# Two-bank PSUM buffers already in the first mixer matmul, weight splits a tile earlier, sums at half pace, one conv-state load

## The chip, the cores and the metric

The kernel runs on one core of a Trainium2 chip. The metric is the device time of one execution in microseconds (us). Below, PE is TensorE (matmuls), DVE is VectorE, ACT is ScalarE, POOL is GpSimd and SP is the engine that issues most DMAs. A DMA can also be issued from the queue of ACT.

## The reference

One layer of a decoder is computed for 1024 prompt tokens and 8 x 4 sample tokens, with T = 1056 columns in all, 1024 features and 4096 hidden features:

```python
xn = rms_norm(x, norm1_g) * (1 + scale1) + shift1
h, b_gate, c_gate, q, k, v, g_conv, g_att = jnp.split(jnp.dot(xn, w_in), split_at, axis=-1)
u = c_gate * h                       # sample rows: the last two rows of state_conv stand ahead
y_conv = conv_w[0] * u_ext[:, 0:ns] + ...
conv_out = jnp.dot(b_gate * y_conv, w_conv_out)
...
attn_out = jnp.dot(o.reshape(nb, ns, D_ATT), w_attn_out)
mixed = jax.nn.sigmoid(g_conv) * conv_out + jax.nn.sigmoid(g_att) * attn_out
x = x + gate1 * jnp.dot(mixed, w_o)                      # output projection
xn2 = rms_norm(x, norm2_g) * (1 + scale2) + shift2
hid = jax.nn.relu(jnp.dot(xn2, w_mlp_in))                # first mixer matmul
x = x + gate2 * jnp.dot(hid * hid, w_mlp_out)            # second mixer matmul
```

## The kernel before

Everything is kept transposed: a tile has 128 features on the partitions and tokens along the row. To keep the precision of f32, each operand is split in a high and a low part, and each product is three matmuls: high by high, high by low and low by high. Raw weights come by DMA (`load_to`, issued on SP). `prep_to` makes the high part `whi` on ACT (L201) and the low part `wlo` on DVE (L208); with `lazy` the low part is put on a list of things due at the next `slot()`, the point after each tile at which pieces of background work are issued too.

The engines work at their own instruction streams, in the order in which the Python code emits them. The order of the work is thus that of the code, and a generator of background work (`bg`) gives up pieces with a cost each (`yield 300`), so many per slot as the `rate` allows.

The stages are, by time: the pair jobs of the conv and the gates (until about 500 us), attention (until 1200), the projections of conv and attention (until 1335), the output projection (`project`, 24 tiles of 24 matmuls with 352 columns, one of 8 feature blocks m by one of three column chunks ch), 12 plain tiles of the first mixer matmul (`plain_tiles`), 14 pair jobs of it, then the second mixer matmul.

A pair job (`pair_job`) computes two blocks of 128 output features by a seven-product scheme. Its seven passes n = 0 to 6 each multiply one combined weight `wprod` (split by ACT L166 and DVE L170, two passes ahead) with one quarter of the columns, in two halves p = 0 and 1 of 12 matmuls of 264 columns. Half 0 writes a PSUM tile `ps_g` (three buffers of one bank each), half 1 a tile `ps_s` (two buffers). After its 12 matmuls each half is read at once: by an ACT copy (L277 in pass 0, L282 in pass 2), by DVE into a sum (L284 in pass 3, L288 in pass 4) or by `fin`, which is a DVE sum (L1565), a relu and a square on ACT (L1566, L1567) in passes 1, 4, 5 and 6. In the code the readers of half 0 stand between the matmuls of half 0 and those of half 1.

After the last pair job `wide_banks` closes the pool of one-bank tiles and opens a pool of four tiles `ps_w` with two banks each; the second mixer matmul (L1738 to L1740) fills both halves of such a tile and then reads it once. That matmul's operands `hh` and `hl` (L1590, L1598) are prepared while the last pair job runs (`warm`).

For the first pair job in the mixer, sums and differences of the normalized input's quarters are formed by `sums`: DVE and POOL subtractions (L343, L344, L348, L350), and splits `th`, `tl` (L366). They run as background work while the plain tiles run.

The sample rows' conv state is loaded by eight small DMAs (L768), two for each of the first pair jobs' conv blocks, from the queue of SP.

Of the kernel before, what the change touches and what calls it, by code (L numbers as in the profile page):

```python
# [9 lines left out]
F32 = mybir.dt.float32  # L10
# [7 lines left out]
P = 128  # L18
T = 1056
NP = 1024  # L20
CH = 352
NCH = 3
KD = 8
NPC2 = NP - 2 * CH
H = 264
# [3 lines left out]
NB = 8  # L29
# [20 lines left out]
class Trunk:  # L50
    def __init__(self, ctx, tc, t):
        self.tc, self.nc, self.t = tc, tc.nc, t
        pool = lambda **kw: ctx.enter_context(tc.tile_pool(**kw))
        self.cp = pool(name="const", bufs=1)
        self.pg = pool(name="pages", bufs=NPG)
        self.ck = pool(name="chunks", bufs=8)
        self.wp = pool(name="weights", bufs=3)
        self.sm = pool(name="small", bufs=3)
        self.px = ExitStack()
        self.pp = self.px.enter_context(tc.tile_pool(name="psum", bufs=1, space=PSUM))  # L60
        self.dp = pool(name="scratch", bufs=1, space=DRAM)
        self.bg = deque()
        self.paced = [deque(), deque()]
        self.pause = [0, 0]
        self.credit = 0.0
        self.rate = 0.0
        self.items = deque()
        self.ready = set()
        self.bias = None
        self.done = False  # L70
        self.work = 0.0
        self.later = []
        self.act_load = 0.0
        self.dve_load = 0.0
# [15 lines left out]
    def wide_banks(self):  # L90
        self.px.close()
        self.pp = self.px.enter_context(self.tc.tile_pool(name="wide", bufs=1, space=PSUM))

    def wide(self):
        return self.pp.tile([P, 2, 512], F32, name="ps_w", tag="ps_w", bufs=4)
# [155 lines left out]
    def pair_job(self, i, fin, after=None):  # L251
        nc = self.nc
        n0 = 7 * self.npair
        self.npair += 1
        s, z = {}, {}
        for n in range(7):
            if n == 1 and i + 1 < len(self.srcs) and len(self.srcs[i + 1]) == 2:
                self.load_to(i + 1)
            if n == 5 and i + 1 < len(self.srcs) and len(self.srcs[i + 1]) == 1:
                self.load_to(i + 1)  # L260
            if n == 5:
                self.prep_to(i + 1)
            self.products_to(min(n0 + n + 3, self.last_prod))
            w = self.prods.popleft()
            if n == 2:
                self.need("T")
            for p in range(2):
                ps = self.bank("s" if p else "g")[:, :H]
                for k in range(4):
                    hi, lo = w[:, k * P:(k + 1) * P], w[:, 512 + k * P:512 + (k + 1) * P]  # L270
                    xh, xl = self.operand(n, k, p)
                    nc.tensor.matmul(ps, hi, xh, start=(k == 0), stop=False)  # L272
                    nc.tensor.matmul(ps, hi, xl, start=False, stop=False)  # L273
                    nc.tensor.matmul(ps, lo, xh, start=False, stop=(k == 3))  # L274
                if n == 0:
                    s[p] = self.chunk("ps_s")[:, :H]
                    nc.scalar.copy(s[p], ps)  # L277
                elif n == 1:
                    fin(0, 0, p, s[p], ps, ALU.add, False)
                elif n == 2:  # L280
                    z[p] = self.chunk("ps_z")[:, :H]
                    nc.scalar.copy(z[p], ps)  # L282
                elif n == 3:
                    nc.vector.tensor_tensor(out=s[p], in0=s[p], in1=ps, op=ALU.add)  # L284
                    nc.gpsimd.tensor_tensor(out=z[p], in0=z[p], in1=s[p], op=ALU.add)  # L285
                elif n == 4:
                    fin(1, 1, p, z[p], ps, ALU.add, False)
                    nc.vector.tensor_tensor(out=s[p], in0=s[p], in1=ps, op=ALU.add)  # L288
                elif n == 5:
                    fin(1, 0, p, s[p], ps, ALU.subtract, True)  # L290
                else:
                    fin(0, 1, p, z[p], ps, ALU.add, True)
                self.slot()
            del w
            if after is not None:
                after(n)

# [32 lines left out]
        k += 4 if n else 0  # L330
        return self.xh[k][:, c0:c0 + H], self.xl[k][:, c0:c0 + H]

    def sums(self):
        nc = self.nc
        self.tt = {}

        def quarters(k):
            return [v.rearrange("p (a t n) -> p a t n", a=2, t=2)[:, :, i] for v in (self.xp[k], self.xp[k + 4]) for i in range(2)]

        for step in range(6):  # L340
            if step < 4:
                b11, b12, b21, b22 = quarters(step)
                nc.vector.tensor_tensor(out=b11, in0=b12, in1=b11, op=ALU.subtract)  # L343
                nc.gpsimd.tensor_tensor(out=b12, in0=b22, in1=b12, op=ALU.subtract)  # L344
                yield 300
            if 1 <= step < 5:
                b11, b12, b21, b22 = quarters(step - 1)
                nc.vector.tensor_tensor(out=b22, in0=b22, in1=b11, op=ALU.subtract)  # L348
                yield 150
                nc.gpsimd.tensor_tensor(out=b21, in0=b22, in1=b21, op=ALU.subtract)  # L350
                yield 150
            k = step - 2
            if k < 0:
                continue
            x = self.xp[k], self.xp[k + 4]
            tt = []
            for i, v in enumerate(x):
                w = 2 * H if k == 3 and i == 0 else T
                h, l = [], []
                for c in range(0, T, w):  # L360
                    for d, n in ((h, "th"), (l, "tl")):
                        d.append(self.page(n, dt=F32R) if w == T else self.half(n, (P, w), F32R))
                    nc.scalar.copy(h[-1], v[:, c:c + w])
                yield 300
                for j, c in enumerate(range(0, T, w)):
                    nc.vector.tensor_tensor(out=l[j], in0=v[:, c:c + w], in1=h[j].bitcast(F32), op=ALU.subtract)  # L366
                tt.append((h, l))
                yield 300
            self.tt[k] = tt
            self.xp[k] = self.xp[k + 4] = None  # L370
        self.ready.add("T")
# [65 lines left out]
    def start(self):  # L437
        nc, t = self.nc, self.t
        c = self.cp
# [21 lines left out]
        self.load_to(0)  # L461
        load_x(2)
        self.load_to(1)
        self.b_ada, self.g1, self.g2 = vec[:, 0:48], vec[:, 48:56], vec[:, 56:64]
        self.cw = vec[:, 64:88].rearrange("p (a k) -> p a k", a=3)
        eps = c.tile([P, 2], F32, name="eps")
# [296 lines left out]
    def conv_h(self, m):  # L763
        u = self.u = [self.page("u", (P, NP + 2)) for _ in range(2)]
        us = self.us = [self.sm.tile([P, NB, 6], F32, name="us", tag="us", bufs=2) for _ in range(2)]
        for i in range(2):
            self.nc.vector.memset(u[i][:, 0:2], 0.0)
            self.nc.sync.dma_start(out=us[i][:, :, 0:2], in_=self.t["state_conv"][:, m + i])  # L768

        def fin(mi, t, p, a, ps, op, last):  # L770
            for dst, sl, four in self.parts(mi, t, p):
                x, y = a[:, sl], ps[:, sl]
                if four:
                    x, y = (v.rearrange("p (b t) -> p b t", t=NT) for v in (x, y))
                self.nc.vector.tensor_tensor(out=dst, in0=x, in1=y, op=op)
        return fin
# [518 lines left out]
    def run(self):  # L1295
        nc, t, c = self.nc, self.t, self.cp
# [51 lines left out]
        while len(jobs[ji]) == 2:  # L1348
            kd, m = jobs[ji]
# [25 lines left out]
        for ji in range(ji, nb):  # L1375
            kd, g, j = jobs[ji]
            for ch in range(NCH):
                s = slice(ch * CH, (ch + 1) * CH)
                ps = self.bank("g")
# [20 lines left out]
        base = nb  # L1400
# [15 lines left out]
        for n, (ch, m) in enumerate(seq):  # L1416
# [5 lines left out]
            ps = self.bank("g")  # L1422
# [15 lines left out]
        mixh, mixl = {}, {}  # L1438
# [3 lines left out]
        for n, (m, ch) in enumerate(seq):  # L1442
            s = slice(ch * CH, (ch + 1) * CH)
            i, x = divmod(m, 2)
# [15 lines left out]
            del ps, y  # L1460
            if x == 0 and ch == 0:
                self.prep_to(base + i + 1)
            if x == 1 and ch == 2:
                self.wt.pop(base + i)
            self.slot()
# [25 lines left out]
        def project(i, m, ch):  # L1491
            s = slice(ch * CH, (ch + 1) * CH)
            load_x1()
            self.prep_to(i + 1, True)
            ps = self.bank("g")
            self.gemm(ps[:, :CH], self.wt[i], range(KD), [(mixh[k, ch], mixl[k, ch]) for k in range(KD)])
            self.residual(x1[m], ps, gate1, m, ch)
            self.later.append((2, lambda: nc.sync.dma_start(out=self.x1_d[m][:, s], in_=x1[m][:, s])))

# [12 lines left out]
        for chs in ((0,), (1,), (2,)):  # L1512
# [6 lines left out]
            def tail(ch):  # L1519
# [12 lines left out]
                    yield 500  # L1532
                self.ready.add(("x2", ch))
                if ch == 2:
                    yield from self.sums()

            self.later.append((5, lambda chs=chs, tail=tail: self.bg.extend(tail(ch) for ch in chs)))
            for m in range(KD):
# [162 lines left out]
        self.rate = 1000.0  # L1701
        self.plain_tiles(base, "x2", hidden)
        self.last_prod = 7 * (self.npair + 2 * NBLK - NG // 2 + 2 * NSB)
        ji = base + NG
        for i in range(NG, 4 * NBLK, 2):
            if i + 6 < 4 * NBLK:
# [3 lines left out]
        for m in range(KD):  # L1710
            at(END - 11 + 2 * m, lambda m=m: load_y1(m))
            if m > 3:
                at(END + 13 + m, lambda m=m: store(m))
        self.wide_banks()
        g = 0
        for i in range(2 * NSB):
            b, x = divmod(i, 2)
# [266 lines left out]
```

## Time and profile before

| | |
|---|---|
| median of 3 runs | 2136.11 us (2134.2 to 2136.56) |
| the profiled execution | 2137.93 us, of which its span from first to last instruction 2136.1 us |
| busy: PE, DVE, ACT, POOL | 2022.3, 1412.4, 996.6, 780.6 us |
| TensorE clock granted, mean | 0.984 of full speed |
| output projection, 1335 to 1437 us | PE busy 95.7 of 102 us |
| plain tiles, 1437 to 1490 us | PE busy 49.2 of 53 us |
| mixer pair jobs, 1490 to 1776 us | PE busy 286 of 286 us |

The span is the time from the first to the last instruction of the execution; the rest of its time lies around it. A busy share is that of the time in which at least one instruction of the engine runs. Matmuls overlap each other, so the spacing of their starts says more than their length.

### The profile page before, as it was taken

To read this page: it belongs to the slowest core of one execution; us is meant where nothing else is said; L and a number is where in the kernel's file an instruction comes from. 1 tells how busy PE (TensorE), PEld (TensorE's weight loads), DVE (VectorE), ACT (ScalarE), POOL (GpSimd) and SP (SyncE) were. 2 spreads that over 40 slices of the span, in tenths; PEclk is the share of its full clock that TensorE was granted. 3 is DMA by queue.
4 is the path that set the end of the run, shared out by engine and by line. 5 is a ranking of instruction groups with operands and counts; after the bars stand their busy time and mean duration, and the time that the engine had idled before them with its cause. 6 is when DMAs were issued, how large, how long until landed. Compare 5 with 4: busy or idle time off the path is not lost. (4 is left out here: it accounts for less than half of the span.)

```text
span 2136.1 us, 38668 instructions
## 1 busy us (share of the span) xinstructions
PE 2022.3 (95%) x15092; PEld 1901.1 (89%) x15092; DVE 1412.4 (66%) x2776; ACT 996.6 (47%) x2165; POOL 780.6 (37%) x544
## 2 busy tenths in 40 slices
PE   5899999999999999999999989999999998999998
PEld 2799999889989888888888889989999998999998
DVE  4847766434667655566676677678444446999998
ACT  4623232434666655555555233455555556433332
POOL 3635655421111111100011114234333335888885
PEclk8899999999999999999999999999999999999999
DMA  7242312664122344333247985642356729555542
GB/s 288 64 144 83 101 51 91 220 233 160 47 65 61 119 130 132 122 126 123 88 141 233 284 261 181 202 158 86 135 192 246 258 102 356 180 202 207 209 149 115
DMA packets 143375, 338.68 MB, mean 159 GB/s; under 512 B 34392, under 2 KB 81112, under 8 KB 142168
## 3 DMA queue, kind: packets, MB, share of 16 engines
q1 hardware_dynamic: 142760, 336.01, 46.8%
q8 instruction: 118, 1.93, 0.4%
q14 instruction: 65, 0.53, 0.1%
q10 hardware_dynamic: 432, 0.20, 0.0%
HBM read 279.00 MB, written 116.39 MB: 185 GB/s over the span
## 5 line engine op out<-in xcount | busy, mean ns | idle before, releaser
L170 DVE TENSOR_TENSOR wprod<-wraw,wprod 128x512 fp32r<-128x512 f32 x276 | 276.0, 1000 | 179.8 <-ACT wprod L166 178.2
L385 PE MATMUL ps_g<-xh,whi 128*128 128x352 f32 x1056 | 357.0, 338 | 8.0 <-DVE graw L107 3.8
L385 PE MATMUL ps_g<-xh,wlo 128*128 128x352 f32 x1056 | 345.8, 328 | 7.2 <-DVE wlo L208 7.2
L385 PE MATMUL ps_g<-xl,whi 128*128 128x352 f32 x1056 | 345.8, 327 | 2.4 <-POOL xl L414 1.5
L1738 PE MATMUL ps_w<-hh,wprod 128*128 128x264 f32 x784 | 225.1, 287 | 13.7 <-DVE acc L1745 7.0
L385 PEld LDWEIGHTS ps_g<-xh,whi 128*128 128x128 f32 x1056 | 202.9, 192 | 32.9 <-issue 13.2
L1739 PE MATMUL ps_w<-hl,wprod 128*128 128x264 f32 x784 | 224.0, 286 | 0.0
L1740 PE MATMUL ps_w<-hh,wprod 128*128 128x264 f32 x784 | 223.9, 286 | 0.0
L166 ACT CAST wprod<-wraw 128x512 fp32r<-128x512 f32 x276 | 163.1, 617 | 123.6 <-DVE wprod L170 91.1
L385 PEld LDWEIGHTS ps_g<-xh,wlo 128*128 128x128 f32 x1056 | 202.4, 192 | 8.5 <-DVE wlo L208 8.5
L385 PEld LDWEIGHTS ps_g<-xl,whi 128*128 128x128 f32 x1056 | 203.4, 193 | 4.9 <-POOL xl L414 3.4
L208 DVE TENSOR_TENSOR wlo<-wraw,whi 128x512 fp32r<-128x512 f32 x200 | 151.7, 798 | 50.8 <-ACT whi L201 50.4
L170 POOL TENSOR_TENSOR lo<-qn,hi 128x1024 fp32r<-128x1024 f32 x12 | 32.9, 2738 | 360.6 <-ACT hi L166 325.0
L1738 PEld LDWEIGHTS ps_w<-hh,wprod 128*128 128x128 f32 x784 | 148.6, 190 | 15.4 <-issue 7.8
L285 POOL TENSOR_TENSOR ps_z<-ps_z,ps_s 128x264 f32<-128x264 f32 x64 | 63.9, 1000 | 255.4 <-DVE ps_s L284 255.3
L1740 PEld LDWEIGHTS ps_w<-hh,wprod 128*128 128x128 f32 x784 | 148.7, 190 | 0.0
L1739 PEld LDWEIGHTS ps_w<-hl,wprod 128*128 128x128 f32 x784 | 148.7, 190 | 0.0
L272 PE MATMUL ps_s<-th,wprod 128*128 128x264 f32 x512 | 146.3, 286 | 1.7 <-DVE ps_s L284 1.7
L272 PE MATMUL ps_g<-th,wprod 128*128 128x264 f32 x512 | 146.7, 287 | 0.0
L274 PE MATMUL ps_g<-th,wprod 128*128 128x264 f32 x512 | 145.9, 285 | 0.0
L273 PE MATMUL ps_s<-tl,wprod 128*128 128x264 f32 x512 | 145.7, 285 | 0.0
L273 PE MATMUL ps_g<-tl,wprod 128*128 128x264 f32 x512 | 145.7, 285 | 0.0
(351 smaller groups left out, 5936.9 us busy)
## 6 DMA issues: line engine op xcount, KB each, us to landing
wraw<-in_w_in SPq DMA_DIRECT2D x76, 512.0 KB, 4.3
wada<-in_w_ada SPq DMA_DIRECT2D x48, 512.0 KB, 5.4
hid_d<-hid SPq DMA_DIRECT2D x32, 528.0 KB, 3.4
wraw<-in_w_mlp_in SPq DMA_DIRECT2D x32, 512.0 KB, 5.8
wraw<-in_w_mlp_out SPq DMA_DIRECT2D x32, 512.0 KB, 3.8
hraw<-hid_d SPq DMA_DIRECT2D x56, 264.0 KB, 4.6
kv<-in_v SPq DMA_DIRECT2D x28, 512.0 KB, 6.1
wraw<-in_w_conv_out SPq DMA_DIRECT2D x24, 512.0 KB, 7.9
```

The source lines that it names most:

```text
L166: nc.scalar.copy(hi, src)
L170: eng.tensor_tensor(out=lo, in0=src, in1=hi.bitcast(F32), op=ALU.subtract)
L208: self.nc.vector.tensor_tensor(out=lo[:, s], in0=w[:, s], in1=hi[:, s].bitcast(F32), op=ALU.subtract)
L272: nc.tensor.matmul(ps, hi, xh, start=(k == 0), stop=False)
L273: nc.tensor.matmul(ps, hi, xl, start=False, stop=False)
L274: nc.tensor.matmul(ps, lo, xh, start=False, stop=(k == 3))
L285: nc.gpsimd.tensor_tensor(out=z[p], in0=z[p], in1=s[p], op=ALU.add)
L385: self.nc.tensor.matmul(ps, a, x, start=(i == 0), stop=(i == n - 1))
L1738: nc.tensor.matmul(ps[:, p], wh, xh, start=(k == 0), stop=False)
L1739: nc.tensor.matmul(ps[:, p], wh, xl, start=False, stop=False)
L1740: nc.tensor.matmul(ps[:, p], wl, xh, start=False, stop=(k == 1))
```

## The change

Five edits:

- In `pair_job` both halves of a pass write one two-bank tile `ps_w` if `self.joint` is set, which `wide_banks` now does. `wide_banks` is called ahead of the mixer's pair jobs, no longer behind them; the pair jobs of the conv stage run with `joint` unset.
- In `project` the weight of tile i + 2 is split in the middle of tile i (`gemm` calls `mid` after 12 of 24 matmuls); before, that of tile i + 1 was split ahead of tile i. One call in the stage before brings the first one.
- `sums` for the last chunk's tail charges its pieces twice the cost, so about half as many are emitted per slot.
- The conv state is loaded once, as `old`, by one DMA on the queue of ACT at the start; DVE copies take the place of the eight small loads.

```diff
     def wide_banks(self):
         self.px.close()
         self.pp = self.px.enter_context(self.tc.tile_pool(name="wide", bufs=1, space=PSUM))
+        self.joint = True
...
+            two = self.wide() if self.joint else None
             for p in range(2):
-                ps = self.bank("s" if p else "g")[:, :H]
+                ps = two[:, p, :H] if self.joint else self.bank("s" if p else "g")[:, :H]
                 for k in range(4):
...
-    def sums(self):
+    def sums(self, f=1):
...
-                yield 300
+                yield 300 * f
...
+        self.old = c.tile([P, KD, NB, 2], F32, name="old")
+        nc.scalar.dma_start(out=self.old, in_=t["state_conv"])
...
-            self.nc.sync.dma_start(out=us[i][:, :, 0:2], in_=self.t["state_conv"][:, m + i])
+            self.nc.vector.tensor_copy(us[i][:, :, 0:2], self.old[:, m + i])
...
+            if x == 1 and ch == 0 and i == 3:
+                self.prep_to(base + i + 2, True)
...
-            self.prep_to(i + 1, True)
             ps = self.bank("g")
-            self.gemm(ps[:, :CH], self.wt[i], range(KD), [(mixh[k, ch], mixl[k, ch]) for k in range(KD)])
+            self.gemm(ps[:, :CH], self.wt[i], range(KD), [(mixh[k, ch], mixl[k, ch]) for k in range(KD)],
+                      lambda: self.prep_to(i + 2, True))
...
-                    yield from self.sums()
+                    yield from self.sums(2)
...
         self.last_prod = 7 * (self.npair + 2 * NBLK - NG // 2 + 2 * NSB)
+        self.wide_banks()
...
-        self.wide_banks()
```

The first place that shows how instructions move is PE in pass n = 1 of a mixer pair job, where half 0 ends and half 1 begins. Names carry the number of their buffer; in brackets stands the engine whose semaphore the instruction waits on. Before:

```order
L272 MATMUL ps_g_17118<-xh_15185,wprod_17031 128x264
L273 MATMUL ps_g_17118<-xl_15193,wprod_17031 128x264
L274 MATMUL ps_g_17118<-xh_15185,wprod_17031 128x264
L272 MATMUL ps_s_17135<-xh_15182,wprod_17031 128x264 [waits DVE_49]
L273 MATMUL ps_s_17135<-xl_15190,wprod_17031 128x264
L274 MATMUL ps_s_17135<-xh_15182,wprod_17031 128x264
```

Half 1 opens another tile than half 0 filled; its wait is on the reader that emptied this buffer of `ps_s` two passes earlier. After:

```order
L275 MATMUL ps_w_17356<-xh_15187,wprod_17271 128x264
L276 MATMUL ps_w_17356<-xl_15195,wprod_17271 128x264
L277 MATMUL ps_w_17356<-xh_15187,wprod_17271 128x264
L275 MATMUL ps_w_17356<-xh_15184,wprod_17271 128x264 [waits DVE_49]
L276 MATMUL ps_w_17356<-xl_15192,wprod_17271 128x264
L277 MATMUL ps_w_17356<-xh_15184,wprod_17271 128x264
```

The same tile now stands on both sides. The wait's counter, followed through the built program, is that of the DVE instruction L1572 that reads half 0 of this same tile `ps_w_17356`, so half 1 begins after that read; in pass n = 0 and 2 the wait is on the ACT copy of half 0 in the same way.

The second place is DVE around that read. Before, in the order in which DVE runs them (the splits of the next products, then the two readers of this pass):

```order
L170 TENSOR_TENSOR wprod_17076<-ws1_17034,wprod_17076 128x512 [waits Activation_49]
L170 TENSOR_TENSOR wprod_17115<-wraw_16850,wprod_17115 128x512 [waits PE_49,Activation_49]
L1565 TENSOR_TENSOR ps_t_17131<-ps_s_17092,ps_g_17118 128x264 [waits PE_49]
L1565 TENSOR_TENSOR ps_t_17148<-ps_s_17108,ps_s_17135 128x264 [waits PE_49]
L170 TENSOR_TENSOR wprod_17152<-wraw_16852,wprod_17152 128x512 [waits DMAHW1_49,DVE_49,Activation_49]
```

After:

```order
L172 TENSOR_TENSOR wprod_17315<-ws1_17274,wprod_17315 128x512 [waits Activation_49]
L172 TENSOR_TENSOR wprod_17353<-wraw_17095,wprod_17353 128x512 [waits Activation_49]
L1572 TENSOR_TENSOR ps_t_17369<-ps_s_17331,ps_w_17356 128x264 [waits PE_49]
L1572 TENSOR_TENSOR ps_t_17385<-ps_s_17346,ps_w_17356 128x264 [waits PE_49]
L172 TENSOR_TENSOR wprod_17389<-wraw_17097,wprod_17389 128x512 [waits DMAHW1_49,DVE_49,Activation_49]
```

The order on DVE is the same; the two readers now read one tile, and the split of a later product still stands ahead of them.

The third place is DVE at the second-quarter sums and the first pair job (L343, L348 are the subtractions, L366 the `tl` splits, L208 the low parts of a plain tile's weight). Before:

```order
L366 TENSOR_TENSOR tl<-x_14843,th 128x1056
L343 TENSOR_TENSOR x_14803<-x_14803 128x2x264
L348 TENSOR_TENSOR x_14923<-x_14923,x_14765 128x2x264
L208 TENSOR_TENSOR wlo<-wraw,whi 128x512 x2
L366 TENSOR_TENSOR tl<-x_14757,th 128x1056
L366 TENSOR_TENSOR tl<-x_14883,th 128x1056
L348 TENSOR_TENSOR x_14963<-x_14963,x_14803 128x2x264
```

After (L346, L351, L369 and L210 are the same lines; the last row is the first reader of the pair jobs):

```order
L351 TENSOR_TENSOR x_14893<-x_14893,x_14767 128x2x264
L210 TENSOR_TENSOR wlo<-wraw,whi 128x512 x2
L369 TENSOR_TENSOR tl<-x_14765,th 128x1056
...
L172 TENSOR_TENSOR wprod<-wraw,wprod 128x512
L369 TENSOR_TENSOR tl<-x_14933,th 128x1056
L172 TENSOR_TENSOR wprod<-ws_16242,wprod 128x512
L369 TENSOR_TENSOR tl<-x_14813,th 128x528 x2
L369 TENSOR_TENSOR tl<-x_14973,th 128x1056
L172 TENSOR_TENSOR wprod<-wraw,wprod 128x512
L1572 TENSOR_TENSOR ps_t<-ps_s,ps_w 128x264 x2
```

The weight's low part moved ahead of two `tl` splits and of two subtractions, and three `tl` splits moved in among the product splits, ahead of the first reader of the pair jobs.

## Rows read from the trace of the kernel before

**Rows 1.** Table by stretch: bounds and length, busy by engine (instructions), clock, DMA share, GB/s.

```profile
1490.00:1776.00 286.00, 285.97 (x2351) 285.75 (x2350) 131.74 (x266) 160.17 (x373) 97.83 (x83) 1.00 0.54 196
1790.00:2081.00 291.00, 283.97 (x2314) 282.35 (x2314) 273.34 (x301) 119.69 (x174) 239.28 (x109) 1.00 0.59 205
```

**Rows 2.** Timeline of all engines, two mixer passes: start, length, engine, line, out<-in [idle before].

```profile
1603.95 0.28 PE L274 MATMUL ps_s<-th,wprod 128*128 128x264 f32 x1
...
1604.28 0.43 DVE L284 TENSOR_TENSOR ps_s<-ps_s 128x264 f32<-128x264 f32 x1 [0.95 <-PE ps_s L274]
...
1605.80 0.43 DVE L1565 TENSOR_TENSOR ps_t<-ps_z,ps_g 128x264 f32<-128x264 f32 x1 [0.50 <-PE ps_g L274]
...
1606.15 0.42 DVE L288 TENSOR_TENSOR ps_s<-ps_s,ps_g 128x264 f32<-128x264 f32 x1
...
1607.27 0.43 DVE L1565 TENSOR_TENSOR ps_t<-ps_z,ps_s 128x264 f32<-128x264 f32 x1 [0.70 <-POOL ws L237]
...
1607.73 0.43 ACT L1566 ACTIVATE ps_t<-ps_t 128x264 f32<-128x264 f32 x1 [0.58 <-DVE ps_t L1565]
...
1608.19 0.42 ACT L1567 ACTIVATE hid<-ps_t 128x264 f32<-128x264 f32 x1
...
1608.52 0.60 ACT L166 CAST wprod<-wraw 128x512 fp32r<-128x512 f32 x1
...
1609.15 0.69 DVE L170 TENSOR_TENSOR wprod<-wraw,wprod 128x512 fp32r<-128x512 f32 x1 [1.12 <-ACT wprod L166]
...
1609.76 0.42 DVE L1565 TENSOR_TENSOR ps_s<-ps_s,ps_g 128x264 f32<-128x264 f32 x1
```

**Rows 3.** Timeline of ACT, end of one pair job and start of the next.

```profile
1615.04 0.60 ACT L166 CAST wprod<-ws 128x512 fp32r<-128x512 f32 x1
1615.55 0.37 ACT L277 COPY ps_s<-ps_g 128x264 f32<-128x264 f32 x1
1615.95 0.38 ACT L277 COPY ps_s<-ps_s 128x264 f32<-128x264 f32 x1
1616.22 0.63 ACT L166 CAST wprod<-wraw 128x512 fp32r<-128x512 f32 x1
```

**Rows 4.** Table of waits, whole span, PE: for whom, us in total, times, longest.

```profile
PE ps_w L1738 <- DVE acc L1745: 7.0, 7, 1.2
```

**Rows 5.** Table by stretch: two stretches at half clock.

```profile
1423.20:1426.60 3.40, 3.40 (x13) 3.40 (x13) 1.87 (x6) 1.83 (x4) 1.20 (x2) 0.50 0.27 75
...
1781.60:1788.40 6.80, 5.26 (x24) 5.29 (x25) 6.80 (x10) 4.64 (x8) 1.66 (x2) 0.50 0.50 173
```

**Rows 6.** Timeline of all engines around the old change of pools.

```profile
1778.63 1.05 ACT L1590 CAST hh<-hraw 128x1056 fp32r<-128x1056 f32 x1
...
1779.71 1.99 DVE L1598 TENSOR_TENSOR hl<-hraw,hh 128x528 fp32r<-128x528 f32 x2 [2.33 <-ACT hh L1590]
...
1782.68 0.42 ACT L1566 ACTIVATE ps_z<-ps_z 128x264 f32<-128x264 f32 x1 [2.48 <-DVE ps_z L1565]
...
1783.14 0.56 PE L1738 MATMUL ps_w<-hh,wprod 128*128 128x264 f32 x1 [6.62 <-ACT ps_z L1566]
```

**Rows 7.** Table of waits of PE, 1335 to 1490 us.

```profile
PE ps_g L385 <- DVE wlo L208: 5.4, 4, 3.6
PE ps_g L385 <- ACT whi L201: 4.3, 5, 1.3
```

**Rows 8.** Timeline of PE in the plain tiles.

```profile
1476.98 0.43 PE L385 MATMUL ps_g<-xh,wlo 128*128 128x352 f32 x1 [3.58 <-DVE wlo L208]
```

**Rows 9.** Timeline of SP's queue, then PE, at the second conv pair job's weights.

```profile
110.59 15.42 SPq L768 DMA_DIRECT2D us<-in_state_conv  x2
126.11 4.22 SPq L188 DMA_DIRECT2D wraw<-in_w_in  x2
...
134.93 0.39 PE L272 MATMUL ps_g<-xh,wprod 128*128 128x264 f32 x1 [3.72 <-ACT wprod L166]
```

More of the change, by code (lines that the diff above doesn't have):

```diff
@@ L59, in __init__ @@
         self.px = ExitStack()
+        self.joint = False
         self.pp = self.px.enter_context(tc.tile_pool(name="psum", bufs=1, space=PSUM))
@@ L293, in pair_job @@
                 self.slot()
-            del w
+            del w, two, ps
             if after is not None:
@@ L348, in sums @@
                 nc.vector.tensor_tensor(out=b22, in0=b22, in1=b11, op=ALU.subtract)
-                yield 150
+                yield 150 * f
                 nc.gpsimd.tensor_tensor(out=b21, in0=b22, in1=b21, op=ALU.subtract)
-                yield 150
+                yield 150 * f
             k = step - 2
@@ L363, in sums @@
                     nc.scalar.copy(h[-1], v[:, c:c + w])
-                yield 300
+                yield 300 * f
                 for j, c in enumerate(range(0, T, w)):
@@ L367, in sums @@
                 tt.append((h, l))
-                yield 300
+                yield 300 * f
             self.tt[k] = tt
```

## The prediction

> **What bounds the kernel now.** I read the table by stretch first. In the mixer's pair jobs PE is busy 285.97 of 286.00 us at full clock [rows 1]: nothing else is on the path there, and every wait put in front of PE is paid in full. One pair job takes 286 / 14 = 20.43 us, a pass 2.92, a half of 12 matmuls 1.46, a matmul 0.122. I then read the timeline of two passes, to see how long a reader takes to hand a tile back. Elsewhere PE waits: the table of waits for 1335 to 1490 us names ACT and DVE as makers of split weights [rows 7], and the timeline shows one long wait where the pools change [rows 6]. So one edit touches a stage that has no idle time to lose, and the others touch waits of some us each.
>
> **Edit 1, both halves in one tile.** The order shows that half 1 of a pass now opens the tile that the reader of half 0 still reads, and the program makes it wait for that read. There are 98 such passes. Let t be the start of the last matmul of the previous pass. Then half 0 starts at t + 0.12, its last matmul at t + 1.46, and half 1 would start at t + 1.58, if it waited for nothing.
>
> The handover: from the last matmul's start to its reader 0.33 (1603.95 to 1604.28), the reader 0.43 on DVE [rows 2] and 0.38 on ACT [rows 3], and from a reader's end to the matmul that waited for it 0.04 (1782.68 + 0.42 to 1783.14) [rows 6], taken as 0.05. So half 1 starts at t + 1.46 + 0.33 + 0.43 + 0.05 = t + 2.27 at the earliest: 0.69 late. The first matmul after a wait is 0.11 longer than the others, 0.43 for 0.32 [rows 8]; I add that for every restart.
>
> That is the floor. The reader is often later still, since DVE and ACT work in order and other work of the last pass stands ahead. Before, this lateness was hidden, as another tile was free: at 1609.76 `fin` reads a half that was long finished [rows 2]. The steps from start to start: `fin` to relu 0.46, relu to square 0.46, square to CAST of the next product 0.33, CAST to its low part on DVE 0.63, low part to `fin` 0.61 [rows 2]; CAST to COPY 0.51, COPY to CAST 0.27 [rows 3]. The start of half 1 in each pass, counted from t:
> - n = 0 and 2: previous `fin` 0.33, relu 0.79, square 1.25, CAST 1.58, COPY 2.09, its end and handover 0.43: 2.52.
> - n = 1 and 3: previous COPY 0.33, CAST 0.60, low part 1.24, reader 1.85, end 0.48: 2.33.
> - n = 4 reads each half twice on DVE, 0.35 apart (1605.80, 1606.15) [rows 2]: 2.27 + 0.35 = 2.62.
> - n = 5 and 6: `fin` 0.33, relu 0.79, square 1.25, CAST 1.58, low part 2.21, `fin` 2.82, end 0.48: 3.30.
>
> The sum over a job is 18.9; each pass then has 11 matmul spacings (1.34) and a restart (0.11), together 10.2. A job so takes 29.1 us, 8.7 more than now, and 14 of them **+121 us**. Lower bound by the floor alone: 98 x (0.69 + 0.11) = +78. Upper bound without the clock: one more low part (0.61) in each pass, +180; I take the chain, as each of its steps is a row.
>
> The order on DVE and ACT isn't changed by this edit, and the bank would be free: half 0 and half 1 lie in different banks. The Trainium skill, PSUM — Partial Sum Buffer, "Summary: rules for kernel authors", says that PSUM may be read while a matmul runs if the matmul targets a different bank, and that semaphores should guard by bank. By that rule the chip itself asks for no wait here and this edit would cost 0; the trace agrees that a read and matmuls in another bank run side by side (1605.80 lies within the matmuls of half 1) [rows 2]. The program, though, guards by tile.
>
> **The clock.** After PE has waited, the granted clock fell to 0.50 for 3.4 us at 1423.20 and for 6.8 us at 1781.60 [rows 5], which is 1.2 of 2.4 GHz. In the first, 13 matmuls of 0.16 us fit where 21 would at full clock: 1.3 us lost, call it 1.5. A wait of 3.58 us went ahead of another such fall [rows 8]; seven waits of up to 1.2 us in the second mixer matmul brought none, its stretch shows 1.00 [rows 1, 4]. The new waits are 0.8 to 1.7 us, the longest in n = 5 and 6, in between the two. I take five falls in all, **+8**, bounded by 0 and two in each job, +42.
>
> **The pools' change moves.** The wait of 6.62 us at 1783.14 [rows 6] and the half clock behind it (5.26 busy us at half speed, 2.6 lost [rows 5]) need no longer be: 9.4 us. But that wait was the late reader of the last half, and the reader is as late as before: in the last pair job `hh` and `hl` stand ahead of the product's low part. Its chain in n = 6: square 1.25, `hh` 1.58, `hl` 1.08 later, low part 1.92 later, `fin` 0.61, end 0.48 [rows 6]: 5.67 instead of 3.30, +2.4, and some 2 more for the work that `warm` puts into n = 5. **-5** (bounds -9.4 and 0). The new change of pools waits for the relu of the last plain tile, one handover of ACT like 0.33 + 0.46: **+0.8**.
>
> **Weights a tile earlier in the output projection.** The waits for `wlo` and `whi` between 1335 and 1490 us are 5.4 and 4.3 [rows 7]; 3.6 of them belong to the plain tiles. Eight waits of 6.1 us remain; each costs 0.16 more than its row, because a row starts with the end of a matmul that is 0.32 long and would be followed after 0.16, and 0.11 for the restart: 8.3. Two falls of the clock follow them (one in [rows 5]), 3. With the split a tile and a half ahead, a tile being 24 x 0.16 = 3.9 us, it has over twice the time; **-11** (bounds -6, when the falls stay or the raw weights land late, and -12).
>
> **Sums at half pace.** `wlo` moves ahead of two `tl` on DVE, so the wait of 3.58 with its restart and its fall of the clock, 5.3 us, goes. Three `tl` now stand ahead of the first reader in the first pair job, where edit 1 makes PE wait for that reader. Between all and nothing I take half: **-2.7**.
>
> **Conv state.** Two small loads hold SP's queue for 15.42 us, and the weights issued behind them at 126.11 come late: PE waits 3.72 at 134.93 [rows 9], with the fall of the clock some 5.5. Issued 15 us sooner, they should land in time, unless the packets of the work ahead of them are still in the engines: **-4.5** (bounds 0 and -5.5). The eight copies on DVE are small and lie in a stage where DVE has slack: if that cover were gone, 1 us.
>
> **The sum.** 121 + 8 - 5 + 0.8 - 11 - 2.7 - 4.5 = +106.6 on 2137.9, the profiled execution: 2244.5. That execution lies 1.8 above the median of the runs, so 2243.
>
> **Rivals.**
> - **Only the floor.** If the chains start earlier than I think, because ACT and DVE run ahead while PE waits, each pass loses 0.8: 2136 + 78 - 22 = 2192. For it: ACT is busy 160 and DVE 132 of 286 us [rows 1]. Against it: a chain starts with the reader of the previous half, and that can't run ahead. Chance 0.10.
> - **The clock stays low for long.** At half clock a matmul takes 5.26 / 24 = 0.22 [rows 5]. Half 1 would start at t + 0.22 + 2.42 + 0.33 + 0.48 = 3.45 and a pass take 5.97; a job 42.1, with the second read of n = 4, 13 us more than 29.1. All 14 jobs would give +182, a third of them +61: 2243 - 8 + 61 = 2296 and up. For it: a pass of 4.2 us holds 2.9 of matmuls. Against it: [rows 1, 4]. Chance 0.11. The Trainium skill, TensorE: Matmul & The Clock Gate, "A second HAM failure mode: psum-queue depth-cycling", tells of a kernel that cycled through PSUM banks, idled shortly between groups, and saw the clock fall and rise again and again; no stretch before shows it.
> - **No wait is paid.** If half 1 does not wait, since the reader is done or the wait is met by an older read, edit 1 costs nothing and the rest gives 9.4 + 11 + 5.3 + 4.5 - 0.8 = 29 less: 2107, faster. It decides from a handover under 0.12 us, the spacing of two matmuls; the rows show 0.8 from the last matmul to a free tile [rows 2, 6]. The rule on banks above is on this side. Chance 0.03.
> - Smaller effects that cancel, within 0.2% of 2136 (4 us, about what a measurement of this kernel can tell from no change): 0.02.
>
> The forecast itself has 0.74, with a range of its own of 2215 to 2275 (the falls of the clock, and the bounds of the gains). **The range** 2190 to 2290 takes in the floor and leaves out most of the clock's case. Slower 0.95, same 0.02, faster 0.03.
>
> **What the new profile would show.** In the mixer's pair jobs waits of PE for ACT's and DVE's readers of `ps_w`, 98 of them, 0.7 to 1.7 us long and longest in n = 5 and 6; a job of 29 us; PE's share there down to 70%. No wait of PE at the start of the second mixer matmul, few between 1335 and 1437, none at 134.9. I would be wrong if the waits were shorter than 0.7, or if the granted clock in the pair jobs were clearly under 1.

## The result, and the profile after

The change made the kernel slower: 2253.93 us, median of 4 runs (2251.78 to 2256.91), against 2136.34 for the kernel before (4 runs). The ratio is 1.0551, 95% interval 1.0528 to 1.0574. The profiled execution took 2256.91, its span 2255.1; that is the slowest of the four runs, 3 us above the median.

The table by stretch of the changed kernel, for 12 pair jobs of the mixer (the second to the thirteenth), for the last one, and for the second mixer matmul behind it; columns as in [rows 1]:

```profile
1516.37:1867.07 350.70, 269.75 (x2019) 252.11 (x2017) 112.42 (x228) 140.32 (x324) 82.90 (x72) 1.00 0.37 135
1867.00:1904.00 37.00, 26.22 (x169) 24.65 (x169) 15.26 (x24) 14.60 (x30) 9.74 (x7) 0.87 0.64 230
1904.00:2195.00 291.00, 283.91 (x2311) 282.30 (x2311) 278.59 (x302) 123.19 (x180) 241.44 (x109) 1.00 0.59 207
```

Against [rows 1]: a stretch in which PE was never idle now has PE busy 269.75 of 350.70 us, 77%. The 12 jobs took 350.7 us, 29.2 each, in place of 20.4. The second mixer matmul, the last row, is what it was: 283.91 of 291 us busy, before 283.97. DVE and ACT do in 350 us the work that they did for 12 jobs in 245.

The waits of PE in the mixer's pair jobs (the engine, tile and line that waits, for whom, us in total, times, longest):

```profile
PE ps_w L275 <- DVE ps_s L1572: 24.6, 14, 3.2
PE ps_w L275 <- DVE ps_z L1572: 19.1, 13, 1.5
PE ps_w L275 <- DVE ps_s L291: 14.2, 14, 2.1
PE ps_w L275 <- ACT ps_s L280: 11.3, 14, 1.4
PE ps_w L275 <- DVE ps_t L1572: 11.0, 14, 3.2
PE ps_w L275 <- ACT ps_z L285: 10.5, 14, 0.8
PE ps_w L275 <- DVE ps_s L287: 8.3, 14, 0.6
PE ps_w L275 <- ACT rl L1556: 0.6, 1, 0.6
```

Before, this table has no row for these jobs. Each reader of a half 0 has its own row with 14 waits, one for each job: the `fin` of n = 5 (`ps_s`, L1572), of n = 6 (`ps_z`), the second read of n = 4 (L291), the copies of n = 0 and 2 (L280, L285), the `fin` of n = 1 (`ps_t`), the sum of n = 3 (L287). The last of `ps_z` lies behind this window. With it they are 98, as many as forecast. The last row of the table is the wait at the new change of pools.

One pass n = 5, in the timeline of all engines; the first row is the start t of the last matmul of the pass before:

```profile
1594.16 0.28 PE L277 MATMUL ps_w<-th,wprod 128*128 128x264 f32 x1
...
1594.55 0.43 DVE L1572 TENSOR_TENSOR ps_t<-ps_z,ps_w 128x264 f32<-128x264 f32 x1 [1.87 <-PE ps_w L277]
...
1595.02 0.42 ACT L1573 ACTIVATE ps_t<-ps_t 128x264 f32<-128x264 f32 x1 [1.76 <-DVE ps_t L1572]
...
1595.47 0.42 ACT L1574 ACTIVATE hid<-ps_t 128x264 f32<-128x264 f32 x1
...
1595.62 0.28 PE L277 MATMUL ps_w<-th,wprod 128*128 128x264 f32 x1
1595.80 0.60 ACT L168 CAST wprod<-wraw 128x512 fp32r<-128x512 f32 x1
1596.44 0.69 DVE L172 TENSOR_TENSOR wprod<-wraw,wprod 128x512 fp32r<-128x512 f32 x1 [1.11 <-ACT wprod L168]
1597.05 0.42 DVE L1572 TENSOR_TENSOR ps_s<-ps_s,ps_w 128x264 f32<-128x264 f32 x1
...
1597.52 0.39 PE L275 MATMUL ps_w<-th,wprod 128*128 128x264 f32 x1 [1.62 <-DVE ps_s L1572]
```

The reader `fin` of half 0 starts at 1597.05, 1.43 us after the half's last matmul at 1595.62. It stands behind the low part of the next product (1596.44), which waits for the CAST (1595.80), which stands behind relu and square of the previous half (1595.02, 1595.47), whose `fin` ran at 1594.55. PE starts half 1 at 1597.52, 3.36 us after t. That is the chain which the prediction laid out from [rows 2, 3], step for step.

The start of half 1 counted from t, the median over 14 jobs in each trace; the last column is the median of the 12 middle jobs:

```
                     n=0   n=1   n=2   n=3   n=4   n=5   n=6   us a job
before               1.59  1.58  1.58  1.59  1.58  1.58  1.59  20.44
predicted            2.52  2.33  2.52  2.33  2.62  3.30  3.30  29.1
measured after       2.51  2.34  2.50  2.34  2.68  3.36  3.29  29.15
split after reader   2.23  2.27  2.23  2.26  2.68  2.26  2.27  26.31
```

(The last line is an experiment, below.)

### The profile page after: what moved, and what is told of

It reads as the page before. It is cut to its first block, busy times and chain, and to the rows that moved or that the text cites. A ratio compares the mean times of both kernels' runs of the same rounds, so it can differ in the third digit from the quotient of the medians.

```text
span 2255.1 us, 38662 instructions
## 1 busy us (share of the span) xinstructions
PE 2052.9 (91%) x15092; PEld 1911.2 (85%) x15092; DVE 1418.8 (63%) x2784; ACT 999.9 (44%) x2165; POOL 785.6 (35%) x544
## 4 chain that ended last, share of the span: by engine, by line
PE 29%; DVE 19%; ACT 7%; issue 4%; DMA 3%; POOL 1%; SPq 0%; DVEq 0%; POOLq 0%; ACTq 0%
PE ps_g L388 14%; DVE wprod L172 5%; DVE acc L1752 4%; PE ps_w L275 4%; PE ps_w L277 2%; PE ps_w L276 2%; ACT wprod L168 2%; DVE hl L1605 2%; DVE wlo L210 1%; DVE ps_t L1572 1%; ACT S L1007 1%; DMA wb<-w_d 1%; PE ps_w L1745 1%; PE ps_w L1747 1%; PE ps_w L1746 1%
## 5 line engine op out<-in xcount | busy, mean ns | idle before, releaser
L275 PE MATMUL ps_w<-th,wprod 128*128 128x264 f32 x448 | 134.8, 301 | 57.7 <-DVE ps_s L1572 24.6
L210 DVE TENSOR_TENSOR wlo<-wraw,whi 128x512 fp32r<-128x512 f32 x200 | 143.2, 757 | 29.0 <-ACT whi L203 28.9
L275 PEld LDWEIGHTS ps_w<-th,wprod 128*128 128x128 f32 x448 | 85.5, 191 | 69.5 <-DVE ps_s L1572 27.6
L275 PE MATMUL ps_w<-xh,wprod 128*128 128x264 f32 x336 | 102.2, 304 | 44.6 <-DVE ps_z L1572 21.8
L203 ACT CAST whi<-wraw 128x512 fp32r<-128x512 f32 x200 | 113.4, 618 | 49.9 <-DMA wraw<-in_w_conv_out 32.5
L1007 ACT ACTIVATE S<-S,ng 128x128 f32<-128x128 f32 (+1 forms) x192 | 84.2, 440 | 113.1 <-DVE ng L1002 113.1
```

Source lines behind the costliest of these rows:

```text
L203: self.nc.scalar.copy(hi[:, s], w[:, s])
L210: self.nc.vector.tensor_tensor(out=lo[:, s], in0=w[:, s], in1=hi[:, s].bitcast(F32), op=ALU.subtract)
L1007: nc.scalar.activation(s, s, AF.Exp, bias=ng[:, hh, i:i + 1], accum_out=sm[:, hh, i:i + 1])
```

## The experiments

Their kernels before were run on the same chip: 2136.97 us (median of 11 runs) for the first four, 2138.08 (23) for the next four, 2139.59 (9) for the last two. Each ratio is to these.

### Edit 1 undone, and edit 1 alone

The first run takes the change and puts `wide_banks` back behind the pair jobs, so `joint` stays unset in them:

```diff
         self.last_prod = 7 * (self.npair + 2 * NBLK - NG // 2 + 2 * NSB)
-        self.wide_banks()
...
+        self.wide_banks()
         g = 0
```

> All of the change but edit 1: the mixer's pair jobs take their halves from the one-bank tiles again and the pools change behind them, as before. Theory (the wait for the reader of half 0 in the same tile is the whole loss): the pair jobs go back to 20.4 us each, and what is left are the other edits, which up to the start of the pair jobs gained 8 us in the profile of the change; the first pair job may lose up to 4 of it to the tl splits: 2128 to 2132. Rival (another edit costs part of the 118 us): above 2137.

Measured: 2125.64 us, ratio 0.9956 (0.9942 to 0.9971), a little under the range that was expected. The 12 middle jobs took 20.50 each; the stretch from the first of them into the last pair job shows PE without a gap:

```profile
1495.80:1757.00 261.20, 261.20 (x2142) 261.20 (x2141) 118.89 (x244) 146.42 (x345) 86.69 (x75) 1.00 0.54 196
```

The second run is the kernel before with nothing but edit 1 (the diff of `wide_banks` and `pair_job` above).

> Edit 1 alone on the kernel before. Theory: 14 jobs of 29.1 us and a last one that is longer, so the loss of the change and the 8 us that the other edits gained: 2136 + 118 + 8 = 2262, between 2255 and 2268. Rival (the loss needs the other edits as well, as the tl splits that now stand in the pair jobs): 2245 or less.

Measured: 2257.43 us, ratio 1.0571 (1.0555 to 1.0588), inside the range that was expected. Its 12 middle jobs:

```profile
1519.50:1868.90 349.40, 267.62 (x2018) 250.00 (x2017) 112.43 (x228) 140.30 (x324) 82.92 (x72) 1.00 0.37 136
```

They took 349.4 us, 29.1 each. Edit 1 alone thus makes a loss as large as that of the change, and without it the change is a gain of 0.3 to 0.6%. The two don't quite add up: +120 and -11 make +109, and the change lost 118. About half of the gap is the first pair job, 28.95 us in this run's trace and 33.75 in the change's, where the sums at half pace put `tl` splits ahead of readers that PE now waits for.

### The pool or the shared tile

Here the early pool and its two-bank tiles stay, but each half takes a tile of its own and uses one bank of it:

```diff
-            two = self.wide() if self.joint else None
+            two = None
             for p in range(2):
-                ps = two[:, p, :H] if self.joint else self.bank("s" if p else "g")[:, :H]
+                ps = self.wide()[:, 0, :H] if self.joint else self.bank("s" if p else "g")[:, :H]
```

> The change, but each half takes a two-bank tile of its own and uses one bank of it. The pool, its early opening and all readers stay. Theory (the shared tile is the cause): no wait of PE for a reader in the pair jobs, 20.4 us each, and no wait at the old change of pools: 2136 - 8 - up to 7 = 2120 to 2130. Rival (the early pool with four tiles instead of five buffers is the cause): waits stay, 2200 or more.

Measured: 2125.38 us, ratio 0.9951 (0.9936 to 0.9965). The stretch of the 12 middle jobs:

```profile
1496.70:1742.70 246.00, 246.00 (x2019) 246.00 (x2018) 110.86 (x229) 137.86 (x325) 83.62 (x72) 1.00 0.53 193
```

No gap, 20.50 a job. The pool, its size and its early opening cost nothing in the pair jobs; that two halves share a tile does.

### Floor or chain

The wait for the same tile stays, but the next product's CAST and low part are issued behind half 0's reader:

```diff
-            self.products_to(min(n0 + n + 3, self.last_prod))
+            self.products_to(min(n0 + n + (2 if self.joint else 3), self.last_prod))
             w = self.prods.popleft()
...
                     fin(0, 1, p, z[p], ps, ALU.add, True)
+                if p == 0 and self.joint:
+                    self.products_to(min(n0 + n + 3, self.last_prod))
                 self.slot()
```

> The change, but in the mixer's pair jobs the next product's CAST and low part are issued behind the reader of half 0, no longer ahead of it. The wait for the same tile stays. Theory (the reader is late because the split stands ahead of it on ACT and DVE): half 1 starts 2.27 to 2.35 after the last matmul of the pass before (2.62 in n = 4) in place of 2.3 to 3.4, a job takes 26.5 instead of 29.1, 2254 - 36 = 2218, between 2210 and 2226. Rival (the handover alone makes the wait, whatever stands ahead): no change, 2254. Rival (the clock makes much of the loss): in between, with the granted clock moved.

Measured: 2211.56 us, ratio 1.0358 (1.034 to 1.0376), 42 below the change. A job took 26.31 (26.5 expected); the starts of half 1 stand in the last line of the table above. The timeline of a pass n = 5 in this run, all engines:

```profile
1607.23 0.43 DVE L1574 TENSOR_TENSOR ps_s<-ps_s,ps_w 128x264 f32<-128x264 f32 x1 [0.61 <-PE ps_w L277]
1607.69 0.42 ACT L1575 ACTIVATE ps_s<-ps_s 128x264 f32<-128x264 f32 x1 [0.51 <-DVE ps_s L1574]
...
1607.72 0.39 PE L275 MATMUL ps_w<-th,wprod 128*128 128x264 f32 x1 [0.52 <-DVE ps_s L1574]
...
1608.48 0.60 ACT L168 CAST wprod<-wraw 128x512 fp32r<-128x512 f32 x1
...
1609.12 0.69 DVE L172 TENSOR_TENSOR wprod<-wraw,wprod 128x512 fp32r<-128x512 f32 x1 [1.46 <-ACT wprod L168]
```

`fin` (1607.23) now runs ahead of CAST (1608.48) and low part (1609.12); PE goes on at 1607.72. So of the 8.7 us that a job lost, 2.8 were the split ahead of the reader; 5.9 are the handover of a shared tile, 0.84 a pass on average (more in n = 4, which reads twice). The stretch of the 12 middle jobs shows the clock at 1.00, as that of the change:

```profile
1507.70:1823.40 315.70, 267.98 (x2018) 250.39 (x2017) 113.51 (x229) 140.21 (x324) 83.63 (x72) 1.00 0.41 150
```

### Both halves first, then the readers

The two-bank tile is shared, but both readers are issued behind the matmuls of both halves:

```diff
+                halves.append(ps)
+                if not self.joint:
+                    read(p, ps)
+            for p in range(2) if self.joint else ():
+                read(p, halves[p])
```

(`read` holds the readers and the `slot` behind each, unchanged.)

> The change with its shared two-bank tiles, but in the mixer's pair jobs both halves' readers are issued behind the matmuls of both halves. The tile is still shared, the pool opens early. Theory (what costs is that a reader stands between two halves of one tile): no wait for half 0's reader, jobs of 20.4 to 20.5 us, and with four tiles of two halves more room at the end of the stage than in the run where each half took its own tile (there 2.8 and 1.0 us of waits for a tile at the start of the second mixer matmul): 2118 to 2125. Rival (a two-bank tile costs by itself, by its banks or its size): above 2200. Rival (readers a half later make PE wait for a tile): jobs of over 21 us, 2135 or more.

Measured: 2124.15 us, ratio 0.9941 (0.9928 to 0.9953). 12 jobs without a gap, 20.50 each:

```profile
1495.30:1741.30 246.00, 246.00 (x2019) 246.00 (x2017) 115.29 (x228) 134.23 (x326) 84.73 (x72) 1.00 0.53 193
```

Neither rival holds: the same tile, pool and readers, in another order, cost no wait. This run also has only 0.2 us of a wait for a tile at the start of the second mixer matmul; what is left there is the split of `wprod`, behind `hh` and `hl` on ACT and DVE:

```profile
PE ps_w L1756 <- DVE wprod L172: 3.8, 4, 1.6
PE ps_w L1754 <- ACT wprod L168: 0.6, 1, 0.6
```

### The small edits, each alone on the kernel before

The conv state's one load:

> The conv state's one load alone on the kernel before. Theory of the prediction: -4.5, 2132; the profiles of three runs with this edit show 4.0 to 4.6 us less up to 210 us. Rival (the packets ahead in the DMA engines hold the weights, not SP's queue, as the profile of the change shows where the first weight load itself took 10 us to issue): -1, 2136.

Measured: 2135.66 us, ratio 0.9985 (0.9974 to 0.9995), 3.2 us less at the ratio's middle and 1.1 to 5.6 by its interval. The theory's 4.5 lies inside, the rival's 1 just outside. In its trace PE's wait there is 0.3 us in place of 3.72.

The weight splits a tile earlier:

> The earlier weight splits of the output projection alone on the kernel before. Prediction: -11, 2126. The profile of the change says less: the two falls of the clock went (3 us) and 6 us of waits, but some 2.5 us of waits on ACT and DVE came in their place: -6, 2131.

Measured: 2129.21 us, ratio 0.9966 (0.9953 to 0.9979), 7.3 us less at the ratio's middle.

The sums at half pace:

> The sums at half pace alone on the kernel before. Prediction: -2.7 with edit 1. Without edit 1 no half of the first pair job waits for the reader of the other half: the wait of 3.6 us and its fall of the clock go (5.3), about 1 us comes back in the first pair job: -4, 2132. Rival (the work only moves): 0, 2136.

Measured: 2133.69 us, ratio 0.9978 (0.997 to 0.9987), 4.7 us less at the ratio's middle. The wait of 3.58 us in [rows 8] is gone in its trace; the first pair job took 21.73 in place of 20.74.

### Two paces, and one try more

On the run with late readers, the background work of the output projection at half the rate, and the three large bias loads further apart:

```diff
         self.ready.discard("T")
-        self.rate = 700.0
+        self.rate = 350.0
...
                 in_=src[:, 0:RW].unsqueeze(1).to_broadcast([8, P, RW]))
-            yield 1000
+            yield 10000
```

> The run with late readers, with two paces changed: the output projection's background work gets half the rate (350 for 700 a slot), and the three big bias loads ahead of the second conv pair job are issued some 10 slots apart. Theory (the waits for whi and wlo that came back in the output projection come from normalization work that stands ahead on ACT and DVE; the wait for the conv weights comes from packets in the DMA engines, not from SP's queue): the projection's 5 us of waits fall to under 2 and the wait near 132 us goes: 2117 to 2121. Rival (the splits are late for another reason, and the conv weights too): 2124, no change.

Measured: 2116.16 us, ratio 0.9884 (0.987 to 0.9898), the fastest of all, 1.2% below the kernel before. The output projection's stretch:

```profile
1330.00:1432.00 102.00, 101.71 (x626) 100.50 (x626) 74.18 (x131) 56.35 (x112) 38.69 (x31) 1.00 0.64 214
```

PE is busy 101.71 of 102 us there, and the time is a little below the range that was expected. And the first weight load of the second conv pair job, in the timeline of SP's queue:

```profile
112.03 0.81 SPq L190 DMA_DIRECT2D wraw<-in_w_in  x2
```

Two loads are issued in 0.81 us, and PE has no wait for them. Both waits went, as the theory asked. The issue and the wait shrank together, though, so this run shows that the bias loads just ahead were the cause, not whether they act through the engines' packets or through the queue.

The last run spreads the second mixer matmul's preparation over all passes of the last pair job:

```diff
         def warm(n):
-            tick(2 * n - 14)
-            tick(2 * n - 13)
+            for e in range(4):
+                tick(4 * n - 28 + e)
...
-            at(-13, lambda q=q: fetch(0, q))
-        prepare(0, -8, 2)
+            at(-28, lambda q=q: fetch(0, q))
+        prepare(0, -23, 4)
```

> As the run with the two paces, and the preparation of the second mixer matmul's operands spread over all passes of the last pair job instead of its second half. Theory (the waits for wprod at the start of the second mixer matmul, some 5 us, come from hh, hl and the combinations that stand ahead of the split on DVE): they shrink by half, 2 to 3 us less than the run with the two paces alone. Rival (pages run out and the loads come late): no change or more.

Measured: 2121.16 us, ratio 0.9913 (0.9899 to 0.9927), so 5 us more than with the two paces alone, where 2 to 3 less was expected: the work now makes PE wait inside the last pair job as well. In the trace a wait of 2.2 us for `wprod` appears there, a fall of the clock (0.50 for 3.4 us) behind it, and that job takes 26.08 us in place of 20.45; the waits for `wprod` at the start of the second mixer matmul stay. The theory of too much work on DVE there isn't refuted, but this was no remedy; whether pages ran short was not tried.

## Why the prediction was right

2243 was forecast and 2253.93 measured: +107 and +118. The mechanism is the one forecast, and its main term was right to 1%.

Set against the profile before, matmul by matmul, the two part ahead of the mixer's pair jobs, not in them. From the first pair job to the end the change lost 126.3 us, where the terms for that part make +126.6 (121 + 8 - 5, and 2.6 for the sums). Up to the first pair job it gained 7.3, where the terms make 20.0. Of the 12.7 between these, 4.4 had come up to 200 us, 3.8 from there to 1330, in stages for which no gain or loss was forecast, and 4.8 in the output projection; the plain tiles came out 0.2 better.

- **Edit 1.** +121 for 14 jobs, 8.7 us each. Measured: 29.15 against 20.44 in an ordinary job, 8.71. The start of half 1 was predicted within 0.07 us in each of the seven passes. The run with the split behind the reader shows that it was right to add the chain to the floor: it takes back only the chain. The floor itself was predicted as 0.80 a pass, 5.6 a job, and measured as 5.9, since n = 4 reads twice.
- **The clock.** +8 for five falls, bounds 0 and 42. The profile shows five in the pair jobs:

```profile
1491.64:1495.04 3.40, 2.92 (x13) 2.92 (x14) 0.42 (x2) 0.85 (x2) 0.00 (x0) 0.50 0.02 5
1686.20:1689.60 3.40, 3.40 (x18) 3.40 (x17) 0.46 (x2) 1.35 (x3) 0.15 (x1) 0.50 0.00 0
1887.58:1890.98 3.40, 3.29 (x16) 2.98 (x14) 1.94 (x3) 2.15 (x4) 0.26 (x1) 0.50 0.90 328
1894.41:1897.81 3.40, 3.40 (x18) 3.40 (x17) 0.43 (x1) 0.93 (x4) 2.94 (x3) 0.50 0.00 0
1901.24:1904.64 3.40, 3.11 (x14) 3.11 (x15) 0.30 (x2) 0.85 (x2) 1.27 (x1) 0.50 0.02 5
```

  One lies in the first job, one in the seventh, three in the last. Half of the busy time at half clock, as the prediction counts it, is 8.1 us; the jobs grew by less, the seventh by 0.95 (30.10 for 29.15). The number five was taken between wide bounds, so that it came out is luck. Where the falls would come was not foreseen: none of the other 11 middle jobs, with waits of up to 1.6 us, has one; the one in the seventh job came behind a wait of 1.97 us, the others at waits of 2.1 to 3.2. The rival of a low clock fell: the middle jobs, with PE busy 77%, show 1.00.
- **The pools' change.** -5, made of 9.4 gained and 4.4 lost again in the last job. The wait of 6.62 us [rows 6] is gone, and the second mixer matmul takes 350.8 us to the end in place of 353.0, since the half clock at its start is gone too. But the last job with its end took 27.22 us before, 37.27 after: +10.05, or 1.3 more than an ordinary job's loss. Here the waits of that job, from the change's table of waits:

```profile
PE ps_w L275 <- DVE ps_s L1572: 3.2, 1, 3.2
PE ps_w L275 <- DVE ps_z L1572: 2.7, 1, 2.7
PE ps_w L275 <- DVE ps_s L291: 2.1, 1, 2.1
```

  These are n = 5, 6 and 4, in an ordinary job 1.6, 1.5 and 0.9, so 4.0 us came back as waits, where the prediction had 2.4 for n = 6 and some 2 for n = 5 and left out n = 4. The rest of what the last job has over an ordinary one (8.1 in all) is some 4.1, by an estimate the three falls of the clock. Counted under the clock, they leave this term near the -5; counted here, they leave it -0.9. In the run where each half has its own tile most of the old wait does go: its last job took 21.34, though a wait of 2.5 us for a tile and 1.0 for split weights follow in the second mixer matmul. The new change of pools was expected to cost 0.8 and cost 0.7: a wait of 0.6, the last row of the table of waits above, and the restart.
- **The output projection.** -11 was too much. The change's trace gains 6.2 between 1330 and 1450 us, and the edit alone 7.3 by time (interval 4.5 to 10). Both falls of the clock went, as forecast. But waits for the same split weights remain in other places:

```profile
PE ps_g L388 <- ACT whi L203: 3.2, 3, 1.8
PE ps_g L388 <- DVE wlo L210: 1.1, 2, 0.7
```

  [rows 7] had 6.1 of them in this stage. That the split has "over twice the time" didn't hold for all tiles; the reading is that the CAST stands in ACT's stream behind normalization work of the background, and the run at half the rate of that work agrees, since it takes nearly all of the rest (0.2 us of waits left).
- **The sums.** -2.7 in all. In the change's trace the wait and its fall of the clock went, 5.4 up to the first pair job, and that job then took 33.75, 4.6 more than an ordinary one; about 1.5 of it is a fall of the clock. Net about -1, or -2.5 with that fall counted under the clock. Alone, without edit 1, they bring 4.7.
- **The conv state.** -4.5, bounds 0 and -5.5. In the change's trace PE still waits 2.72 us in place of 3.72 [rows 9]:

```profile
112.54 10.58 SPq L190 DMA_DIRECT2D wraw<-in_w_in  x2
```

```profile
134.80 0.39 PE L275 MATMUL ps_g<-xh,wprod 128*128 128x264 f32 x1 [2.72 <-ACT wprod L168]
```

  The small loads are gone from SP's queue, and the first weight load now takes the 10 us that the first small one took. So the reason given (two small loads hold the queue) was wrong for most of their time: whatever stands there waits, with the bias loads just issued ahead. The weights' issue ends 7 us sooner (123.12 for 130.33), not 15. The size of the term fared better than the change's own profile says. Without this edit the wait is 2.4 to 3.7 us in four profiles. With it, and the bias loads where they were, it is 0.3 to 1.2 in five, and the change's 2.72 is the exception; those five gain 4.1 to 5.0 us on the kernel before at this place, the change 1.0, and three runs without the edit 0.4 to 1.3. Spreading the bias loads removed the wait.

The signs that the prediction named: PE's share in the middle jobs fell to 77%, and no wait stands at the start of the second mixer matmul. The waits of n = 1 and 3 show 0.6 in the table of waits, under the 0.7 that was to count against it. The table counts from the end of the last matmul, which lasts 0.28; counted in starts, as the prediction's sum does, half 1 is 0.75 late there (2.34 for 1.58 or 1.59), as forecast.

The rivals: the floor alone would have given 2192, no wait 2107, a long low clock 2296; the per-pass starts tell each of them apart from what happened. The rule of the Trainium skill, PSUM — Partial Sum Buffer, "Summary: rules for kernel authors", which asks for a different bank and a guard by bank, wasn't contradicted by any run: with a tile for each half, reads ran beside matmuls in another bank and the jobs took 20.50 us, without a wait. What made PE wait was the program's guard, which goes by tile.

The profile of the change also has 2 us more near 480 us, at small matmuls that no edit touches. They appear in some runs and not in others, that of the sums alone among them; their cause stays open.

## What to carry to other kernels

If two accumulation groups share a tile, the program guards by tile, and a reader stands between them, the second group waits for the reader, even in another bank; put the readers behind both groups, or give each its own tile. The price isn't only the handover but all that stands ahead of the reader on its engine: work that was hidden because nobody waited for that reader becomes part of the matmul engine's path. And a wait removed at the end of a stage is only gone when what was late isn't waited for elsewhere.

## What the runs showed of the hardware

- Waits of 0.6 to 1.6 us in each pass of 4.2, PE busy 77% over 350 us, left the granted clock at 1.00, but for one fall to 0.50 for 3.4 us behind a wait of 1.97. In the last job, with waits of 2.1, 3.2 and 2.7 us, it fell to 0.50 and rose again three times, a mean of 0.87.
- The issue of a DMA on SP's queue took 10 us behind the third of three large strided loads, and did so for a small load before and for a 512 KB load after; with the loads further apart two such issues took 0.81.
